# Stores of ScalarE's results and of the block inverses, issued from ScalarE's DMA queue instead of SyncE's

## The chip, the cores and the metric

The kernel runs on one core of a Trainium2 chip. The metric is the time of one execution on the device in microseconds (us), the median of several runs. The core has five engines with instruction streams of their own: TensorE (PE, matrix products), VectorE (DVE), ScalarE (ACT), GpSimd (POOL) and SyncE (SP). Here SyncE does nothing but start DMA transfers. A DMA is an instruction of the engine whose queue issues it: it stands in that engine's order, waits there for what it reads or overwrites, and so holds what stands behind it on that engine.

## The reference

One layer over 512 latent tokens and 256 context tokens, all in float32 with a model width of 1024. A half-step feed-forward block stands at either end; between them stand two parallel mixers, merged by sigmoid gates:

```python
x = ffn_sublayer(x, mod_x, 0, ffn1_w_in, ffn1_w_out)          # post_ln(a*x + 0.5*gate*swiglu(modulate(x)))
ctx = ffn_sublayer(ctx, mod_c, 0, ffn1_w_in, ffn1_w_out)
qa, ka, va, qkv_b, z_b, a_b, b_b, ga, gb = split_proj(modulate(x, shift_x, scale_x) @ w_in)
...
o_a = na_latent(grid(qa), grid(ka), grid(va), kc_h, vc_h, na_rpb)     # 8 heads, 8x16 window and all context keys
o_ctx2, s_ctx = gated_delta_chunks(*gdn_prepare(qkv_c, ...), s0, update_ctx)   # 4 heads x 2 directions
o_lat2, _ = gated_delta_chunks(*gdn_prepare(qkv_b, ...), s_ctx, True)          # chunks of 64 tokens
o_b = gdn_output(o_lat2[0] + jnp.flip(o_lat2[1], axis=2), z_b, gdn_norm_w)
y = sigmoid(ga) * (o_a @ w_pa) + sigmoid(gb) * (o_b @ w_pb)
x = post_ln(a * x + gate_x * (y @ w_o), ln_g[1], ln_b[1])
x = ffn_sublayer(x, mod_x, 2, ffn2_w_in, ffn2_w_out)
```

The recursion (`gated_delta_chunks`) is what the change lies beside. For each chunk it solves a unit lower triangular system, (I + m) uw = rhs with m from `k_beta @ k.T * decay`, and then passes a 128x128 state from chunk to chunk.

## The kernel before

Products with weights are made as three fp32r matmuls of split operands: the high part of the weight `wh` (a cast on ScalarE, L129), its low part `wl` (VectorE, L130), and the activations' parts `uxh` and `uxl` (L183 to L185). The raw weights `wr` are loaded by SyncE some steps ahead (L165).

The order of instructions on each engine is not written out: the program is written in the tile framework, whose scheduler orders every engine's instructions by a timeline of its own from the dependences. A DMA moved from one queue to another is thus planned anew, and other instructions may come out in another order too.

The stretch from about 760 to 1040 us holds the recursion. Its systems are handled in three blocks of two steps (`bi` 0, 1, 2). For each:

- `gram` loads the decays `Dt` (L908, VectorE L911, exponential on ScalarE L912), has the products k k^T and q k^T made by `products`, and forms `Bt` (VectorE L917), which SyncE stores to DRAM as `bd` (L918), and `At` (L921). For steps 2 and 3 `products` copies each product out of PSUM on ScalarE (`kq`, L891), uses it, and stores it to DRAM as `kqd` (L892), from which steps 4 and 5 and the mirrored direction read it again (L896); two `kq` buffers exist.
- `base_inverse` reads the 32x32 diagonal blocks back from `bd`, 64 at once (`Ltr` and `L`, L937), brings one half into order on ScalarE (L938), and inverts them in 31 dependent steps of a product and a reduction on VectorE (`bt` L944, `Xt` L945). Four DMAs store the result to DRAM as `rd` (L949).
- `inverse` loads `rd` again, in another layout, as `T0` and `T1` (L966; the profile calls both `T`), and joins 32x32 blocks to 64x64 and 128x128 by small matmuls (`mm`, L847, into the PSUM tiles `pi`), with copies between them on VectorE (`Y` L988 and L1015, `T` L1004) and ScalarE (L979, L1005, L1023).
- `scan_step` passes the state on: `r`, `vn`, `S`, and the outputs `oacc`.

These steps depend on one another, so they leave TensorE free between. It is filled with the projections of the attention and the gates: the list `FILLS` holds 28 tiles of `qa`, `ka`, `va` (4 each), `ga` and `gb` (8 each), and `turn` hands out quarters of them after each step by the rates `RATE`. Each tile is made by `fill_spill`: 24 matmuls into a PSUM bank (`pm`, two of them), one ScalarE instruction that brings it to `spill` (L595 for qa, L597 for ka and va, L599 for ga and gb, two buffers), and a store of 256 KB to DRAM (L603). The tile `z` is made in the same function, earlier, with a further VectorE instruction.

After the third block `gdn_out` normalizes the recursion's output, turns it on TensorE (L850) and writes it through ScalarE (`vn`, L1107) to `obd` (L1108). `attend` then makes the attention and combines: it loads `ob` from `obd` (L1265) and `z` (L1267).

Of the kernel before, what the change touches and what calls it, by code (L numbers as in the profile page):

```python
# [57 lines left out]
def body(ctx, tc, I, out, dbg=None):  # L58
    nc = tc.nc
# [499 lines left out]
    obd = tl(dp, [4, P, NX], "obd")  # L559
# [25 lines left out]
    def fill_spill(p, name, m, dst, parts=1):  # L585
        w = win_w(name, m)
        px = tl(pm, [P, NX], *PMB)
        for k in range(KT):
            if k and k % (KT // parts) == 0:
                yield  # L590
            mm3k(px[:], w[0], w[1], uxh, uxl, k)
        t = tl(p, [P, NX], "spill", 2)
        if name == "qa":

            S.activation(t[:].rearrange("p (b r c) -> p r b c", b=4, c=16), px[:].rearrange("p (r b c) -> p r b c", b=4, c=16), AF.Copy, scale=0.125)  # L595
        elif name in ("ka", "va"):
            S.copy(t[:], px[:])  # L597
        else:
            S.activation(t[:], px[:], AF.Tanh, scale=0.5)  # L599
        if name == "z":  # L600

            V.scalar_tensor_tensor(t[:], t[:], 1.0, px[:], op0=ALU.add, op1=ALU.mult)
        nc.sync.dma_start(dst[m], t[:])  # L603
        yield


# [271 lines left out]
    def products(p, s):  # L878

        def one(n, a, o):  # L880
            if s == 1:
                return [kk01[p][:, m ^ 2] for m in range(4)]
            if s < 4:
                t = tl(pgq, [P, 4, P], "pq", 2)
                for m, (d, c, i) in enumerate(mats_of(s)):
                    mm(t[:, m, :], kT[2 * p + i][:, c], a[2 * p + i][:, c - o], start=True, stop=True)
                if s == 0:
                    kk01[p] = t
                else:
                    u = tl(gb_, [P, 4, P], "kq", NKQ)  # L890
                    S.copy(u[:], t[:])  # L891
                    nc.sync.dma_start(kqd[n, s - 2, p], u[:].rearrange("p m c -> p (m c)"))  # L892
            else:
                t = tl(gb_, [P, 4, P], "kq", NKQ)
                for h in range(2):
                    nc.sync.dma_start(t[:, 2 * h:2 * h + 2].rearrange("p m c -> p (m c)"), kqd[n, 5 - s, p, :, 256 * (1 - h):256 * (2 - h)])  # L896
# [28 lines left out]
    def base_inverse(bd, rd):  # L925


        L = tl(gb_, [P, 32, 32], "L")
        tr = tl(gb_, [64, 32, 32], "Ltr")
        Xt = tl(gb_, [P, 16, 32], "Xt", 2)  # L930
        G.memset(Xt[:], 0.0)
        for q in range(4):
            G.memset(Xt[32 * q:32 * q + 32].rearrange("p c k -> p (c k)")[:, q % 2:512:34], 1.0)
        st = 32 * P + 32
        for q in range(4):
            dst = tr[32 * q:32 * q + 32] if q < 2 else L[32 * q:32 * q + 32]
            nc.sync.dma_start(dst, bass.AP(bd.tensor, bd.offset + (q // 2) * 8 * MSTR, [[st, 32], [P, 32], [1, 32]]))  # L937
        S.copy(L[0:64].rearrange("p r c -> p c r"), tr[:])  # L938

        G.memset(L[:].rearrange("p r c -> p (r c)")[:, 0:1024:33], -1.0)  # L940
        for i in range(1, 32):
            c = (i + 1) // 2
            t = tl(gb_, [P, 16, 32], "bt")
            V.tensor_tensor(t[:, 0:c, 0:i + 1], L[:, i:i + 1, 0:i + 1].to_broadcast([P, c, i + 1]), Xt[:, 0:c, 0:i + 1], ALU.mult)  # L944
            V.tensor_reduce(Xt[:, 0:c, i], t[:, 0:c, 0:i + 1], AX, ALU.add, negate=True)  # L945
            if i % 4 == 0:
                yield
        for q in range(4):
            nc.sync.dma_start(bass.AP(rd.tensor, rd.offset + (q // 2) * 32 * 1024 + (q % 2) * 32, [[1024, 32], [64, 16], [1, 32]]),  # L949
                              Xt[32 * q:32 * q + 32])  # L950
        yield

# [138 lines left out]
    def gdn_out(p):  # L1091

        oacc = oaccs[p]
        for t2 in range(2):
            o = oacc[:, 2 * t2:2 * t2 + 2].rearrange("p t i c -> p (t i) c")
            sq = tl(gq, [P, 4, P], "r", 2)
            S.activation(sq[:], o, AF.Square)
            ss = tl(gq, [P, 4], "ss", 2)
            V.tensor_reduce(ss[:], sq[:], AX, ALU.add)
            rs = rsqrt_eps(gq, ss[:], 4, 1.0 / 128.0)  # L1100
            V.tensor_tensor(o, o, rs[:, :, None].to_broadcast([P, 4, P]), ALU.mult)
        for i in range(2):
# [4 lines left out]
            S.activation(o, ps[:].rearrange("p t c -> p (t c)"), AF.Copy, scale=nw[:, 0:1])  # L1107
            nc.sync.dma_start(obd[2 * p + i], o)  # L1108

    Sst = [None, None]  # L1110
    res, rds, inv = {}, {}, {}
# [565 lines left out]
```

## Time and profile before

| | us |
|---|---|
| median of 3 runs | 1548.15 |
| lowest and highest | 1546.49, 1550.94 |
| profiled execution, its time | 1550.49 |
| profiled execution, its span | 1548.7 |
| busy: TensorE | 1469.7 (95%) |
| busy: VectorE | 1049.7 (68%) |
| busy: ScalarE | 604.2 (39%) |
| busy: GpSimd | 230.7 (15%) |
| mean granted clock of TensorE | 0.986 |

The busy times come from one profiled execution. In the rows below, a row of the timeline holds its start, its duration, the engine, the line of the kernel, the operation, output and inputs by their names in the program, and the number of instructions that the row groups; the bracket is the idle time of the engine ahead of it and what ended it. `SPq` and `ACTq` are the queues from which SyncE and ScalarE issue DMAs; the duration of such a row is the issue, not the transfer. A row of the waits holds who waited for whom: the total in us, the number of times, the longest one.

### The profile page before, as it was taken

The page shows a single profiled execution, that of the slowest core. Times are in us where ns is not written, and L with a number is a line of the kernel's source. Part 1 is how long each engine was busy: PE and PEld are TensorE (multiplying, and loading weights), DVE is VectorE, ACT ScalarE, POOL GpSimd, SP SyncE. Part 2 cuts the span into 40 slices and gives each one's busy share as a digit, 9 for nine tenths or more (in the row PEclk, how much of TensorE's full clock was granted, in tenths as well). Part 3 has the DMA queues.
Part 4 walks back from the last instruction along what each step waited for, and adds up shares of the span by engine and source line. Part 5 has one row for each costly group of instructions (what it writes and reads, how often), then busy time and mean ns, then how long its engine had stood idle before and what let it go on. Part 6 is the DMA issues. An engine that isn't in the chain of part 4 may idle for free.

```text
span 1548.7 us, 23667 instructions
## 1 busy us (share of the span) xinstructions
PE 1469.7 (95%) x9221; PEld 1259.6 (81%) x9221; DVE 1049.7 (68%) x1792; ACT 604.2 (39%) x1005; POOL 230.7 (15%) x224
## 2 busy tenths in 40 slices
PE   6999999999999999999996899999999999999997
PEld 4779988888888888898874677866677999998886
DVE  8666762577555397768667886666668599887426
ACT  5434321212112245645533344356516454344310
POOL 0000000000000021223301001266432022220001
PEclk9999999999999999999998999999999999999999
DMA  9566563656555533222476534274353133334422
GB/s 323 196 202 206 179 200 98 190 177 207 191 184 180 191 109 127 92 92 86 131 201 183 163 103 120 76 259 127 100 183 135 60 110 123 109 95 151 136 82 82
DMA packets 107586, 230.72 MB, mean 149 GB/s; under 512 B 34177, under 2 KB 47825, under 8 KB 107473
## 3 DMA queue, kind: packets, MB, share of 16 engines
q1 hardware_dynamic: 105312, 221.79, 45.0%
q10 hardware_dynamic: 1586, 5.32, 0.9%
q0 software_dynamic: 576, 2.10, 0.4%
q8 instruction: 72, 1.18, 0.3%
q14 instruction: 40, 0.33, 0.1%
HBM read 206.33 MB, written 22.85 MB: 148 GB/s over the span
## 4 chain that ended last, share of the span: by engine, by line
PE 62%; DMA 15%; DVE 13%; issue 5%; ACT 3%; POOL 1%; SPq 1%; DVEq 0%; ACTq 0%; POOLq 0%
PE ps L202 19%; DMA wr<-in_w_adaT_dram 7%; PE pm L183 5%; PE ps L185 5%; PE ps L183 5%; PE ps L184 5%; PE pm L185 5%; PE pm L184 4%; DVE wl L130 3%; PE ps L1464 3%; PE ps L1466 3%; PE ps L1465 2%; PE pc L847 2%; DVE adap L272 2%; DMA wr<-in_up_dram 1%
## 5 line engine op out<-in xcount | busy, mean ns | idle before, releaser
L130 DVE TENSOR_TENSOR wl<-wr,wh 128x1024 fp32r<-128x1024 f32 (+1 forms) x215 | 263.5, 1230 | 172.0 <-ACT wh L129 171.2
L129 ACT CAST wh<-wr 128x1024 fp32r<-128x1024 f32 (+1 forms) x215 | 217.6, 1017 | 339.6 <-PE ps L202 77.0
L272 DVE SCALAR_TENSOR_TENSOR adap<-wr,crow 128x1024 f32<-128x1024 f32 x112 | 137.0, 1223 | 90.3 <-DMA wr<-in_w_adaT_dram 88.7
L183 PE MATMUL ps<-uxh,wh 128*128 128x512 f32 (+1 forms) x496 | 182.6, 370 | 4.1 <-ACT wh L129 3.9
L185 PE MATMUL ps<-uxh,wl 128*128 128x512 f32 (+1 forms) x496 | 182.3, 368 | 4.3 <-DVE wl L130 4.2
L184 PE MATMUL ps<-uxl,wh 128*128 128x512 f32 (+1 forms) x496 | 181.2, 366 | 1.1 <-DVE uxl L130 1.0
L108 POOL TENSOR_TENSOR rs<-ve,mhalf 128x1 f32<-128x1 f32 (+2 forms) x46 | 52.4, 1142 | 765.0 <-DVE ve L104 762.1
L183 PE MATMUL pm<-uxh,wh 128*128 128x512 f32 x320 | 132.1, 413 | 4.3 <-ACT spill L599 2.3
L185 PE MATMUL pm<-uxh,wl 128*128 128x512 f32 x320 | 127.4, 398 | 0.9 <-DVE wl L130 0.9
L184 PE MATMUL pm<-uxl,wh 128*128 128x512 f32 x320 | 126.4, 395 | 0.0
L185 PEld LDWEIGHTS ps<-uxh,wl 128*128 128x128 f32 x496 | 94.8, 191 | 23.2 <-DVE wl L130 8.6
L183 PEld LDWEIGHTS ps<-uxh,wh 128*128 128x128 f32 x496 | 94.8, 192 | 20.8 <-ACT wh L129 6.7
L184 PEld LDWEIGHTS ps<-uxl,wh 128*128 128x128 f32 x496 | 95.3, 192 | 15.7 <-DVE uxl L130 1.6
L183 PE MATMUL ps<-uch,wh 128*128 128x256 f32 x352 | 98.6, 280 | 0.0
L185 PE MATMUL ps<-uch,wl 128*128 128x256 f32 x352 | 98.3, 279 | 0.0
L184 PE MATMUL ps<-ucl,wh 128*128 128x256 f32 x352 | 98.3, 279 | 0.0
L202 PE MATMUL ps<-wh,hx 128*128 128x512 f32 x352 | 94.8, 389 | 0.0
L202 PEld LDWEIGHTS ps<-wh,hx 128*128 128x128 f32 x352 | 65.9, 188 | 13.6
L183 PEld LDWEIGHTS pm<-uxh,wh 128*128 128x128 f32 x320 | 61.0, 191 | 16.2 <-ACT spill L599 3.2
L185 PEld LDWEIGHTS pm<-uxh,wl 128*128 128x128 f32 x320 | 60.9, 190 | 15.4 <-DVE wl L130 2.2
L129 ACT CAST hx<-fs 128x512 fp32r<-128x512 f32 x22 | 13.6, 620 | 151.0 <-DVE fs L265 151.0
L184 PEld LDWEIGHTS pm<-uxl,wh 128*128 128x128 f32 x320 | 61.0, 191 | 10.3
(411 smaller groups left out, 3494.8 us busy)
## 6 DMA issues: line engine op xcount, KB each, us to landing
wr<-in_w_adaT_dram SPq DMA_DIRECT2D x88, 512.0 KB, 4.3
wr<-in_up_dram SPq DMA_DIRECT2D x80, 512.0 KB, 3.4
wr<-in_dn_dram SPq DMA_DIRECT2D x58, 512.0 KB, 3.5
wr<-in_win_dram SPq DMA_DIRECT2D x52, 512.0 KB, 3.9
rb<-in_up_dram SPq DMA_DIRECT2D x18, 512.0 KB, 4.3
wr<-in_w_o_dram SPq DMA_DIRECT2D x8, 512.0 KB, 3.9
ac<-in_up_dram SPq DMA_DIRECT2D x6, 512.0 KB, 5.3
Dt<-gcd SPq DMA_DIRECT2D x12, 256.0 KB, 5.6
```

The source lines that it names most:

```text
L108: G.tensor_tensor(rs[:], ve[:], mhalf[:, 0:n], ALU.pow)
L129: S.copy(hi, src)
L130: V.tensor_tensor(lo, src, hi.bitcast(F32), ALU.subtract)
L183: T.matmul(ps, a, uh[:, k, :], start=(k == 0), stop=False)
L184: T.matmul(ps, a, ul[:, k, :], start=False, stop=False)
L185: T.matmul(ps, b, uh[:, k, :], start=False, stop=(k == nk - 1))
L202: T.matmul(banks[t][d][:, c0:c1], a[:, sl], b[:, d * 512 + c0:d * 512 + c1], start=first and j == 0, stop=last and j == 2)
L272: V.scalar_tensor_tensor(pr[:], raw[:], 1.0, crow, op0=ALU.mult, op1=ALU.mult, accum_out=col[:, c:c + 1])
L847: last[0] = T.matmul(*a, **k).ins
L1464: T.matmul(ps[:], a, uh[:, k], start=k == 0, stop=False)
L1465: T.matmul(ps[:], a, ul[:, k], start=False, stop=False)
L1466: T.matmul(ps[:], b, uh[:, k], start=False, stop=k == 3)
```

## The change

Four kinds of DMA are issued by ScalarE (`nc.scalar`) that SyncE (`nc.sync`) issued before. What they read and where they write is the same.

```diff
     if name == "z":
         V.scalar_tensor_tensor(t[:], t[:], 1.0, px[:], op0=ALU.add, op1=ALU.mult)
-    nc.sync.dma_start(dst[m], t[:])
+
+    (nc.sync if name == "z" else nc.scalar).dma_start(dst[m], t[:])
     yield
...
     S.copy(u[:], t[:])
-    nc.sync.dma_start(kqd[n, s - 2, p], u[:].rearrange("p m c -> p (m c)"))
+    nc.scalar.dma_start(kqd[n, s - 2, p], u[:].rearrange("p m c -> p (m c)"))
...
     for q in range(4):
-        nc.sync.dma_start(bass.AP(rd.tensor, rd.offset + ..., [[1024, 32], [64, 16], [1, 32]]),
+        nc.scalar.dma_start(bass.AP(rd.tensor, rd.offset + ..., [[1024, 32], [64, 16], [1, 32]]),
                           Xt[32 * q:32 * q + 32])
...
     S.activation(o, ps[:].rearrange("p t c -> p (t c)"), AF.Copy, scale=nw[:, 0:1])
-    nc.sync.dma_start(obd[2 * p + i], o)
+    nc.scalar.dma_start(obd[2 * p + i], o)
```

These are 28 stores of `spill`, 8 of `kq`, 12 of `Xt` (three blocks of four) and 4 of `vn`: 52 DMAs. The first, second and fourth kind store what ScalarE wrote just before; `Xt` is written by VectorE. By the added blank line, the lines from L603 on have a number higher by one in the changed kernel.

The change moves other instructions as well. On SyncE's queue, around the first block inverse, stood before (`Xt_1245` and `rd0` are the first block's inverse, `T1` and `T0` its reload, `L_1365` and `Ltr_1366` the second block's systems, `kq_1438` and `kq_1442` products of the third):

```order
L937 DMA L_1365_7591<-bd1_1277_7043 32x32x32 x2
L949 DMA rd0_1222_6801<-Xt_1245_6934 512x1x32 x4
L603 DMA gbd_894_4996<-spill_1341_7404 128x512
L165 DMA wr_1359_7559<-in_win_dram 128x1024
L896 DMA kq_1438_7951<-kqd_1208_6729 128x256
L966 DMA T1_1347_7433<-rd0_1222_6801 128x4x32
L966 DMA T0_1346_7432<-rd0_1222_6801 128x4x32
L966 DMA T1_1385_7654<-rd0_1222_6801 128x4x32
L966 DMA T0_1384_7653<-rd0_1222_6801 128x4x32
L896 DMA kq_1438_7951<-kqd_1208_6729 128x256
L896 DMA kq_1442_7970<-kqd_1208_6729 128x256 x2
```

At the same place of SyncE's queue stands now:

```order
L909 DMA Dt_1440_7962<-gcd_892_4994 128x2x256
L897 DMA kq_1438_7951<-kqd_1208_6729 128x256
L938 DMA L_1365_7591<-bd1_1277_7043 32x32x32 x2
L897 DMA kq_1438_7951<-kqd_1208_6729 128x256
L165 DMA wr_1359_7559<-in_win_dram 128x1024
L897 DMA kq_1442_7970<-kqd_1208_6729 128x256 x2
L967 DMA T1_1347_7433<-rd0_1222_6801 128x4x32
L967 DMA T1_1385_7654<-rd0_1222_6801 128x4x32
L967 DMA T0_1346_7432<-rd0_1222_6801 128x4x32
L967 DMA T0_1384_7653<-rd0_1222_6801 128x4x32
```

The stores of `rd0` and of the spill are gone from it, and the four `T` loads have moved behind the loads of `kq_1438` and `kq_1442`. On ScalarE stands at that place now:

```order
L599 ACTIVATE spill_1341_7404<-pm_1337_7369 128x512
L129 CAST wh_1343_7409<-wr_1342_7407 128x1024
L604 DMA gbd_894_4996<-spill_1341_7404 128x512
L939 COPY L_1365_7591<-Ltr_1366_7592 64x32x32
L950 DMA rd0_1222_6801<-Xt_1245_6934 512x1x32 x4
L913 ACTIVATE Dt_1440_7962<-Dt_1440_7962 128x512
```

The `rd0` stores have come between the copy of `L_1365`, which waits for `Ltr_1366`, and the exponential of `Dt_1440`; before, the same rows stood there without the two DMA rows and with the cast ahead of the spill. On VectorE, some 20 us later, around the copy `Y6` that TensorE waits for, stood before:

```order
L945 TENSOR_REDUCE Xt_1367_7593<-bt_1406_7827 128x10
L944 TENSOR_TENSOR bt_1407_7830<-L_1365_7591,Xt_1367_7593 128x11x22
L945 TENSOR_REDUCE Xt_1367_7593<-bt_1407_7830 128x11
L944 TENSOR_TENSOR bt_1408_7833<-L_1365_7591,Xt_1367_7593 128x11x23
L945 TENSOR_REDUCE Xt_1367_7593<-bt_1408_7833 128x11
L917 SCALAR_TENSOR_TENSOR Bt_1436_7942<-kq_1437_7943,beta_897_5004,Dt_1435_7935 128x128
L944 TENSOR_TENSOR bt_1409_7836<-L_1365_7591,Xt_1367_7593 128x12x24
L917 SCALAR_TENSOR_TENSOR Bt_1436_7942<-kq_1437_7943,beta_897_5004,Dt_1435_7935 128x128
L1015 COPY Y6_1363_7572<-pi_1357_7541 128x256
L917 SCALAR_TENSOR_TENSOR Bt_1436_7942<-kq_1437_7943,beta_897_5004,Dt_1435_7935 128x128 x2
```

and stands now:

```order
L945 TENSOR_TENSOR bt_1406_7827<-L_1365_7591,Xt_1367_7593 128x10x21
L918 SCALAR_TENSOR_TENSOR Bt_1436_7942<-kq_1437_7943,beta_897_5004,Dt_1435_7935 128x128 x2
L946 TENSOR_REDUCE Xt_1367_7593<-bt_1406_7827 128x10
L1016 COPY Y6_1363_7572<-pi_1357_7541 128x256
L918 SCALAR_TENSOR_TENSOR Bt_1436_7942<-kq_1437_7943,beta_897_5004,Dt_1435_7935 128x128 x2
L918 SCALAR_TENSOR_TENSOR Bt_1441_7969<-kq_1442_7970,beta_897_5004,Dt_1440_7962 128x128 x4
L945 TENSOR_TENSOR bt_1407_7830<-L_1365_7591,Xt_1367_7593 128x11x22
```

`Y6` has moved ahead of five instructions of the second block's inversion (`bt_1407` to `bt_1409`). At the second `Y6` of this block, some 20 us later, it is four in the same way.

More of the change, by code (lines that the diff above doesn't have):

```diff
@@ L948, in base_inverse @@
         for q in range(4):
[L949 removed]
+            nc.scalar.dma_start(bass.AP(rd.tensor, rd.offset + (q // 2) * 32 * 1024 + (q % 2) * 32, [[1024, 32], [64, 16], [1, 32]]),
                               Xt[32 * q:32 * q + 32])
```

## The prediction

> **What bounds the kernel now.** I read the page first (engine totals, chain), then the stretch in which the moved stores lie (760 to 1040 us) by windows, then TensorE's idle gaps and who ended them, then SyncE's queue around each gap.
>
> ```profile
> PE 1469.7 (95%) x9221; PEld 1259.6 (81%) x9221; DVE 1049.7 (68%) x1792; ACT 604.2 (39%) x1005; POOL 230.7 (15%) x224
> 800.00:830.00 30.00, 28.34 (x139) 23.14 (x138) 26.64 (x69) 12.69 (x19) 0.00 (x0) 1.00 0.64 197
> 830.00:860.00 30.00, 15.03 (x159) 10.84 (x157) 21.18 (x69) 9.97 (x18) 5.08 (x14) 0.77 0.57 148
> 860.00:890.00 30.00, 24.91 (x243) 20.07 (x244) 23.56 (x56) 9.15 (x21) 0.00 (x0) 0.94 0.63 181
> 890.00:920.00 30.00, 28.95 (x330) 23.75 (x329) 25.43 (x86) 15.74 (x35) 3.33 (x9) 1.00 0.44 110
> ```
>
> The columns of the windows are length, busy time of TensorE, its weight loads, VectorE, ScalarE and GpSimd, granted clock, DMA share, GB/s. TensorE is 95% busy over the span, but half idle in 830 to 860, at a granted clock of 0.77. ScalarE is busy 10.0 us of those 30, and at most 15.7 in the other rows, so it has room for issues. What idles TensorE:
>
> ```profile
> 846.92 0.69 PE L847 MATMUL pi<-T,Bt 32*32 32x32 f32 x32 [14.58 <-DMA T<-rd]
> 860.74 0.68 PE L847 MATMUL pi<-Tt,Y 64*64 64x64 f32 x16 [1.14 <-DVE Y L1015]
> 875.37 0.68 PE L847 MATMUL pi<-T,Bt 64*64 64x64 f32 x16 [1.42 <-DVE T L1004]
> 881.22 0.68 PE L847 MATMUL pi<-Tt,Y 64*64 64x64 f32 x16 [2.92 <-DVE Y L1015]
> 953.67 0.45 PE L847 MATMUL pi<-T,Bt 32*32 32x32 f32 x32 [0.85 <-DMA T<-rd]
> 955.24 1.26 PE L847 MATMUL pc<-r,Tt 128*128 128x128 f32 x8 [1.12 <-DVE r L1046]
> 958.81 0.42 PE L847 MATMUL pi<-Y,T 32*32 32x32 f32 x28 [0.91 <-DVE Y L988]
> 1021.47 0.82 PE L1245 MATMUL pt<-ident,pr 128*128 128x128 f32 x4 [1.78 <-POOL pr L1241]
> ```
>
> The bracket is the idle time before the row and who ended it. One stall is large: TensorE stands 14.58 us until the first block inverse has been stored (rd<-Xt) and read back (T<-rd). The rest are gaps of 0.9 to 2.9 us, mostly behind VectorE. SyncE's queue and VectorE around the large one:
>
> ```profile
> 832.66 0.69 DVE L945 TENSOR_REDUCE Xt<-bt 128x16 f32<-128x512 f32 x1
> 833.26 1.22 DVE L130 TENSOR_TENSOR wl<-wr,wh 128x1024 fp32r<-128x1024 f32 x1
> 833.59 1.48 SPq L937 DMA_DIRECT2D L<-bd  x2
> 833.76 1.94 ACT L938 COPY L<-Ltr 64x1024 f32<-64x1024 f32 x1 [4.17 <-DMA Ltr<-bd]
> 835.17 5.17 SPq L949 DMA_DIRECT2D rd<-Xt  x4
> 842.71 2.02 SPq L966 DMA_DIRECT2D T<-rd  x4
> 844.77 4.87 SPq L896 DMA_DIRECT2D kq<-kqd  x3
> 842.71 3.86 DMA T<-rd
> 834.09 5.72 DMA L<-bd
> ```
>
> (The last two are rows of the chain of waits.) The inverse is complete at 833.35. Its four stores occupy SyncE from 835.17 to 840.34; 2.4 us later the loads start, and the first lands at 846.57. So 9.4 us pass between the last reduction and the first load's issue, and this is the only place where the store's queue itself lies on TensorE's path for long.
>
> What SyncE waits for in 760 to 1015 us:
>
> ```profile
> SPq L603 <- ACT spill L597: 38.1, 5, 14.2
> SPq L603 <- ACT spill L595: 23.7, 4, 8.9
> SPq L603 <- ACT spill L599: 21.2, 4, 13.1
> SPq L892 <- ACT kq L891: 8.5, 3, 3.6
> SPq L949 <- DVE Xt L945: 7.4, 1, 7.4
> SPq L1108 <- ACT vn L1107: 1.3, 3, 0.8
> ```
>
> These 100.2 us are SyncE's waits for what the moved stores read; of the engines, only those that need a load queued behind them pay. No weight load appears among what ScalarE or TensorE waits for in this stretch, so most of the 100 us cost nothing.
>
> **The change part by part.** Issue prices, minimum/median/maximum in ns:
>
> ```profile
> L500 ACTq DMA_DIRECT2D x1d<-ax x4: 326/330/336, 546.8 to 576.6; - x4
> L949 SPq DMA_DIRECT2D rd<-Xt x12: 561/624/3163, 835.2 to 941.4; - x12
> L1108 SPq DMA_DIRECT2D obd<-vn x4: 319/320/753, 1004.5 to 1012.7; - x4
> ```
>
> *Issues on ScalarE.* 28 stores of spill, 8 of kq and 4 of vn at 0.33 us, and 12 of rd at 0.62 us: 40 x 0.33 + 12 x 0.62 = 20.6 us, taken off SyncE and put on ScalarE over about 280 us. The cover is ScalarE's idle half. Where a copy of a PSUM bank is queued behind a store and TensorE waits for that copy, 0.33 us each time is paid; I take two such places and a few tenths in the attention part: +0.8 us. Bounds: 0 (all hidden) to +3, if the rd stores hold ScalarE as long as 5.17 us in one place.
>
> *First inverse.* On ScalarE the four rd stores stand behind the 1.94 us copy of L (833.76 to 835.70), so they cannot start earlier than on SyncE (835.17) unless the copy does; Ltr is now loaded ahead of fewer other issues, and I take them at about 834 to 838, a little sooner than 835.17 to 840.34. On SyncE the T loads now stand behind the loads of kq, the last of which reuses a buffer that VectorE's product At must first release. Before, that same kq load sat behind T and its wait is in the 4.87 us row. At needs L's landing (5.72 us after the issue, to 839.8) only through the rows queued ahead of it on VectorE; it is then done near 841, and T is issued near 842 where it was 842.71. One T tile of the first pair comes third instead of second, which gives back up to 0.5. Result -0.9 us; bounds -7 (T issued as soon as rd has landed) and +4 (below).
>
> *860 to 882.* VectorE now runs Y and the Bt products ahead of five and four Xt steps. The Xt steps passed:
>
> ```profile
> 858.37 0.42 DVE L944 TENSOR_TENSOR bt<-L,Xt 128x253 f32<-128x253 f32 x1
> 858.83 0.42 DVE L945 TENSOR_REDUCE Xt<-bt 128x11 f32<-128x253 f32 x1
> 877.50 0.58 DVE L944 TENSOR_TENSOR bt<-L,Xt 128x406 f32<-128x406 f32 x1
> 879.34 0.62 DVE L944 TENSOR_TENSOR bt<-L,Xt 128x450 f32<-128x450 f32 x1
> ```
>
> Five at 0.42 is 2.1 us, which covers the 1.14 us gap; four at 0.6 is 2.4, which leaves about half of the 2.92 gap, since kq loads also have to land (bound: all, or nothing). With the 1.42 gap that is -4.0 us, and another -0.5 for matmuls that run at a lower clock after each idle (0.94 in this window against 1.00 later).
>
> *Second inverse.*
>
> ```profile
> 894.91 2.08 SPq L966 DMA_DIRECT2D T<-rd  x4
> 894.91 4.64 DMA T<-rd
> ```
>
> Before, T landed at 899.55, just when TensorE asked for it. TensorE would now ask 5.4 us earlier (0.9 + 4.0 + 0.5). The inverse itself ends earlier by the Xt steps' own shift, about 3.4 us. So a new gap of 2.0 us opens: +2.0. Bounds 0 and +5.4 (the copy of L, queued ahead of the stores on ScalarE, holds them as long as SyncE did).
>
> *Third inverse.*
>
> ```profile
> 946.88 7.67 DMA T<-rd
> 1013.56 5.30 DMA z<-zd
> ```
>
> The last T load was issued at 946.88 behind five attention loads and a store, and took 7.67 us; gaps of 0.85 + 1.12 + 0.91 = 2.9 follow. TensorE's row for it now stands a dozen rows later, behind fill matmuls, so I take two thirds: -2.0, bounds 0 and -2.9.
>
> *End.* The obd stores leave 0.9 us of SyncE ahead of the ob and z loads (z at 1013.56, landing after 5.30 us, on the chain). I take -0.6 of it, bounds -1.8 (the gap at 1021.47) and +1, since ScalarE's store stands behind a square that it must run first.
>
> Sum: +0.8 - 0.9 - 4.5 + 2.0 - 2.0 - 0.6 = -5.2 us. The profiled execution took 1550.49 (span 1548.7), 2.3 over the median of the three runs, 1548.15; 1550.49 - 5.2 = 1545.3 in its terms, 1548.15 - 5.2 = 1543.0 against the median.
>
> **A rule that speaks against it.** The rows: 52 issues at 0.32 to 0.62 us, against landings of 3.86 to 7.67 us. The Trainium skill, page "DMA: Bandwidth & Descriptors", section "Issuing engines are not separate DMA queues", says that DMAs begun by any engine share the same 16 DMA engines, and that a second initiator saves only sequencer time, "usually small relative to the DMA itself". No run yet shows two initiators in this stretch. By that rule the time would be that of the second rival below, 1546 to 1548, where the sum gives 1543.0.
>
> **Rivals.**
> 1. *More: the T loads go as soon as rd has landed.* Nothing on ScalarE holds rd, it is issued by 836 and down by 839, and T goes at 839 instead of 842.71, so the 14.58 us stall shrinks by 3.7 at least, with the rest as above: 1543.0 - 3 - 2 (no gap at the second inverse) - 2 = about 1536. Against it: the kq loads ahead of T on SyncE.
> 2. *Nothing: the transfers set the pace, not the queue.* Of the 100.2 us that SyncE waits, TensorE sees none but the rd stall, where SyncE merely trades rd's 5.17 us for another wait; VectorE's earlier rows are paid back at the second T load (which must wait for 4.64 us of transfer anyway). 0 to -2: 1546 to 1548. It holds if T<-rd is issued at 842 to 843 again and TensorE's gaps only move.
> 3. *Slower: T behind kq behind VectorE.* If L or the first kq half lands as late as the 7.67 us row (against 5.72), At is done near 843, T is issued near 844.5 and lands at 848.4: the first stall grows by 1.9, VectorE's whole later order shifts by as much, and at the second inverse ScalarE's stores behind the copy of L add 3: +5, 1553. It decides from the point where At ends after 841.5.
>
> **How the numbers follow.** Forecast (1538.5 to 1547, two thirds of it below 1543.5) 0.50; rival 1 0.14; rival 2 0.20; rival 3 0.16. A measurement here can tell about 0.3%, 4.6 us. Faster than 1543.5: 0.50 x 0.66 + 0.14 = 0.47. Same: 0.17 + 0.19 = 0.36. Slower: 0.17, with the worst of rival 2's spread. The range for 8 in 10 leaves out the far ends of rivals 1 and 3: 1534 to 1552.
>
> **What would show it.** Right: T<-rd issued near 842 or earlier and the first stall at 13 to 14 us; the gaps at 860, 875 and 881 gone or halved; a gap of about 2 us before the second inverse's matmuls; ScalarE's queue with rd issues of about 0.6 us each. Wrong: a first stall of 15 us or more, a rd issue on ScalarE that waits for microseconds while copies of PSUM wait behind it, or new gaps of TensorE behind ScalarE's spill copies. It would also be wrong if the order of the attention part, which moves by some rows, costs or gains over 2 us.

## The result and the profile after

The changed kernel takes 1564.69 us (median of 4 runs, 1562.16 to 1569.20), the kernel before 1549.55 us (4 runs, 1546.49 to 1553.37): the ratio is 1.0086, 95% interval [1.0056, 1.0115]. By the ratio it is 13 us slower (9 to 18; the medians differ by 15.1), where 1543.0 was forecast and 1534 to 1552 was the range. The profiled execution took 1563.78 us, with a span of 1562.0 us (before 1548.7).

The page's totals of the changed kernel:

```profile
PE 1480.4 (95%) x9221; PEld 1269.3 (81%) x9221; DVE 1048.8 (67%) x1792; ACT 604.3 (39%) x1005; POOL 227.4 (15%) x224
```

Every engine runs as many instructions as before. TensorE is busy for 10.7 us more (1469.7 before) and idle for 2.6 us more (81.6 against 79.0); the mean granted clock is 0.981 (0.986 before). The four windows that the prediction read and two others, in the changed kernel (length, busy time of TensorE, weight loads, VectorE, ScalarE, GpSimd, then granted clock, DMA share, GB/s):

```profile
800.00:830.00 30.00, 28.86 (x144) 23.37 (x143) 24.64 (x73) 11.48 (x17) 0.00 (x0) 1.00 0.61 206
830.00:860.00 30.00, 15.94 (x162) 11.74 (x161) 23.28 (x69) 9.24 (x17) 4.40 (x14) 0.77 0.69 167
860.00:890.00 30.00, 27.17 (x255) 21.94 (x253) 24.61 (x60) 12.08 (x25) 0.00 (x0) 0.94 0.61 183
890.00:920.00 30.00, 28.14 (x298) 22.94 (x296) 23.26 (x78) 14.62 (x33) 3.31 (x9) 1.00 0.43 108
970.00:1000.00 30.00, 28.76 (x295) 25.65 (x291) 14.66 (x36) 6.32 (x17) 4.28 (x6) 0.89 0.08 27
1110.00:1140.00 30.00, 24.76 (x134) 18.68 (x133) 14.71 (x18) 12.47 (x22) 10.44 (x7) 0.89 0.32 89
```

Windows at the same times do not hold the same work, since the recursion began 3.1 us later in this profile. Counted from its start (65 to 125 us), TensorE is busy for 43.1 of the 60 us around the first inverse, for 39.9 before and for 41.5 in a second profile of before (E9, below): it does more in the same time, as forecast. The prediction did not read the last two windows. In the kernel before they are:

```profile
970.00:1000.00 30.00, 29.90 (x280) 26.82 (x279) 18.15 (x41) 7.22 (x16) 5.70 (x9) 1.00 0.19 67
1110.00:1140.00 30.00, 27.43 (x125) 21.07 (x122) 24.73 (x27) 13.25 (x19) 11.42 (x8) 1.00 0.45 141
```

There the granted clock falls from 1.00 to 0.89; counted by the work it is the same (0.90 at 200 to 235 us behind the recursion's start, 0.89 in the tail defined below, 1.00 in both before). TensorE's gaps in the changed kernel, from the timeline (the bracket: idle time before the row, and who ended it):

```profile
849.75 0.65 PE L848 MATMUL pi<-T,Bt 32*32 32x32 f32 x32 [14.06 <-DMA T<-rd]
881.33 0.68 PE L848 MATMUL pi<-Tt,Y 64*64 64x64 f32 x16 [2.69 <-DVE Y L1016]
961.22 0.45 PE L848 MATMUL pi<-T,Bt 32*32 32x32 f32 x32 [0.28 <-DMA T<-rd]
968.30 0.68 PE L848 MATMUL pi<-T,Bt 64*64 64x64 f32 x16 [0.99 <-DVE T L1005]
969.60 0.68 PE L848 MATMUL pi<-Tt,Y 64*64 64x64 f32 x16 [0.62 <-DVE Y L1016]
971.46 2.08 PE L848 MATMUL pc<-r,Tt 128*128 128x128 f32 x8 [0.80 <-ACT Tt L1024]
1029.66 0.55 PE L1215 MATMUL pt<-ident,vst 128*128 128x128 f32 x3 [1.81 <-ACT pT L1248]
1036.86 1.02 PE L1257 MATMUL po<-pT,vw 128*64 128x128 f32 x7 [2.17 <-ACT pT L1248]
1059.81 1.12 PE L1215 MATMUL pt<-ident,vst 128*128 128x128 f32 x4 [2.32 <-ACT pT L1248]
1128.48 0.79 PE L183 MATMUL pm<-oah,wh 128*128 128x512 f32 x1 [3.12 <-ACT wh L129]
```

The gaps of 1.14 and 1.42 us at 860 and 875 have gone; the stall is 14.06 us (14.58 before). New ones stand at 968 to 971, where two joins of the third inverse and the product that takes their result (`Tt`) come close behind one another, in the attention (1029 to 1060), and at 1128, behind a cast of a weight.

Where the time went by stages, in the profiled executions. The *recursion* runs from the first `pq` product to the last `vn` activation, the *attention* to the last copy of `oa`, the *tail* to the first product with `w_o` (`ps<-wh,yh`). The four rows of before and the four of after:

```profile
765.39 1.05 PE L847 MATMUL pq<-kT 128*128 128x128 f32 x8
1011.36 1.27 ACT L1107 ACTIVATE vn<-pc,nw 128x512 f32<-128x512 f32 x2 [1.81 <-PE pc L850]
1110.86 0.69 DVE L1258 COPY oa<-po 128x512 f32<-128x512 f32 x1 [6.58 <-PE po L1256]
1136.61 0.62 PE L202 MATMUL ps<-wh,yh 128*128 128x512 f32 x2
```

```profile
768.46 1.05 PE L848 MATMUL pq<-kT 128*128 128x128 f32 x8
1016.81 1.27 ACT L1108 ACTIVATE vn<-pc,nw 128x512 f32<-128x512 f32 x2 [1.76 <-PE pc L851]
1119.74 0.69 DVE L1259 COPY oa<-po 128x512 f32<-128x512 f32 x1 [6.59 <-PE po L1257]
1149.63 0.62 PE L202 MATMUL ps<-wh,yh 128*128 128x512 f32 x2
```

| us | start | recursion | attention | tail | rest |
|---|---|---|---|---|---|
| before | 765.4 | 246.0 | 99.5 | 25.8 | 412.1 |
| after | 768.5 | 248.4 | 102.9 | 29.9 | 412.4 |

Recursion +2.4, attention +3.4, tail +4.1, rest +0.3, and 3.1 ahead of the changed stretch. The last is chance: a second profile of the kernel before (E9) began the recursion at 770.1. E9 also tells how far one profile can be trusted for a stage: recursion 243.3 against 246.0 and attention 97.0 against 99.5, the same program.

Of the 10.7 us that TensorE is busy for more, 3.1 lie ahead of the recursion and 1.2 behind the tail. The recursion has 4.1 of them (and 1.7 us less of idle time), the attention 0.1 (3.4 us more of idle time), the tail 2.4 (1.8 us more of idle time). E9's total is 1466.4, 3.3 less than the other profile of the same program.

### The profile page after: what moved, and what is told of

Read it like the earlier page. It is cut to its first block, busy times and chain, and to the rows that moved or that the text cites. A ratio compares the mean times of both kernels' runs of the same rounds, so it can differ in the third digit from the quotient of the medians.

```text
span 1562.0 us, 23639 instructions
## 1 busy us (share of the span) xinstructions
PE 1480.4 (95%) x9221; PEld 1269.3 (81%) x9221; DVE 1048.8 (67%) x1792; ACT 604.3 (39%) x1005; POOL 227.4 (15%) x224
## 4 chain that ended last, share of the span: by engine, by line
PE 57%; DMA 18%; DVE 14%; issue 5%; ACT 3%; POOL 1%; SPq 1%; ACTq 0%; DVEq 0%; POOLq 0%
PE ps L202 17%; DMA wr<-in_w_adaT_dram 7%; PE ps L185 4%; PE ps L183 4%; PE ps L184 4%; PE pm L183 4%; PE pm L184 4%; PE pm L185 4%; PE ps L1467 3%; PE ps L1466 3%; PE ps L1465 3%; DVE wl L130 3%; PE pc L848 2%; DVE adap L272 2%; DMA Dt<-gcd 2%
## 5 line engine op out<-in xcount | busy, mean ns | idle before, releaser
L184 PEld LDWEIGHTS ps<-uxl,wh 128*128 128x128 f32 x496 | 94.9, 191 | 15.3 <-DVE uxl L130 1.2
L202 PEld LDWEIGHTS ps<-wh,hx 128*128 128x128 f32 x352 | 65.9, 188 | 14.5 <-DVE fs L265 0.6
```

The lines of the kernel that those rows point to most:

```text
L184: T.matmul(ps, a, ul[:, k, :], start=False, stop=False)
L202: T.matmul(banks[t][d][:, c0:c1], a[:, sl], b[:, d * 512 + c0:d * 512 + c1], start=first and j == 0, stop=last and j == 2)
```

## The experiments

Two things change at once: the queue of 52 stores, and the order in which the scheduler sets other instructions. The experiments separate them. The queue is made a parameter, and an order can be imposed: the program is planned once for other queues, and each engine's instructions are then chained in that plan's order by dependences that only order, and make nobody wait.

```diff
+    queue = lambda kind: nc.scalar if kind in moved else nc.sync
...
+        (nc.sync if name == "z" else queue("spill")).dma_start(dst[m], t[:])
...
+def keep(tc, order):
...
+    last = {}
+    for name, engine in order:
...
+        if engine in last:
+            tc.add_manual_dep(i, last[engine], ..., reason="order")
+        last[engine] = name
```

`MOVED` are the stores on ScalarE's queue, `ORDER_OF` those of the plan whose order is kept. `TAKE` mixes two plans: the order of `BASE`, but in the named pieces (engine, from row to row) that of `OTHER`. *Old order* is the plan with all stores on SyncE, *new order* that of the changed kernel. The line numbers of these kernels are higher by 4 or 5 than those of before. A median is of 5 to 12 executions, beside 23 to 35 of the kernel before.

| | kernel | median us | ratio, 95% interval | recursion | attention | tail |
|---|---|---|---|---|---|---|
| E1 | SyncE, new order | 1562.49 | 1.0084 [1.0056, 1.0111] | 248.3 | 101.4 | 29.4 |
| E2 | ScalarE, old order | 1551.09 | 1.0001 [0.9984, 1.0018] | 240.9 | 100.9 | 25.8 |
| E3 | only rd on ScalarE, planned freely | 1556.79 | 1.0037 [1.0022, 1.0053] | 241.7 | 105.3 | 29.1 |
| E4 | all but rd on ScalarE, planned freely | 1566.27 | 1.0097 [1.0074, 1.0119] | 249.4 | 101.8 | 30.7 |
| E5 | E2 + new tail | 1551.59 | 1.0013 [0.9997, 1.0030] | 242.8 | 98.7 | 28.8 |
| E6 | E2 + new attention | 1556.11 | 1.0048 [1.0029, 1.0067] | 241.1 | 106.1 | 25.9 |
| E7 | E2 + new inverses and scan | 1552.46 | 1.0024 [1.0006, 1.0041] | 248.5 | 97.5 | 25.8 |
| E8 | after + two places in the old order | 1558.51 | 1.0074 [1.0050, 1.0099] | 250.6 | 103.3 | 27.6 |
| E9 | before again | 1548.27 | 0.9999 [0.9982, 1.0016] | 243.3 | 97.0 | 25.6 |
| E10 | old order, rd and kq on ScalarE | 1548.40 | 1.0001 [0.9983, 1.0019] | 245.0 | 97.8 | 25.8 |
| E11 | E2 + new third inverse and scan | 1552.37 | 1.0023 [0.9999, 1.0048] | 244.6 | 102.3 | 28.1 |
| E12 | E6, spill and vn stores on SyncE | 1552.17 | 1.0024 [1.0005, 1.0043] | 241.4 | 103.0 | 27.5 |
| E13 | E2 + new attention, TensorE alone | 1555.83 | 1.0037 [1.0022, 1.0052] | 241.0 | 107.4 | 25.4 |
| E14 | E2 + new attention, all but TensorE | 1555.12 | 1.0032 [1.0014, 1.0050] | 241.5 | 104.7 | 25.8 |
| E15 | E2 + new first two inverses | 1553.16 | 1.0018 [0.9998, 1.0039] | 247.6 | 98.9 | 25.8 |

The stage columns are of the one profiled execution; E13's took 1560.21 us, the slowest of its twelve runs.

### Queue or order: E1 and E2

```diff
 E1: +MOVED = ()                              +ORDER_OF = ('kq', 'obd', 'rd', 'spill')
 E2: +MOVED = ('kq', 'obd', 'rd', 'spill')    +ORDER_OF = ()
```

> All 52 stores are back on SyncE's queue, but every other instruction of each engine is kept in the order that the changed kernel has. Theory O (the loss is the new order of the other instructions): as slow as the changed kernel, 1558 to 1567 us, with the third block's rd stores near 948 and TensorE's wait of about 3 us for a weight cast near 1128. Theory Q (the loss is ScalarE's queue: stores that hold ScalarE or come later from it): back at the kernel before, 1547 to 1552.

> All 52 stores on ScalarE's queue, but every other instruction of each engine is kept in the order that the kernel before has. Theory O: no slower than before, 1543 to 1551 us; the four T loads of the first inverse no longer stand behind any store on SyncE and can go when rd has landed, so that the 14.6 us stall should shrink by 1 to 4 us. Theory Q: 1558 to 1567.

E1 has none of the 52 stores on ScalarE's queue and is as slow as the changed kernel: 1.0084 against 1.0086; its wait for the weight cast is 2.94 us, at 1128.73. E2 has all of them there, in the old order, and is as fast as before. Both times are those of theory O (E2's 1551.09 at the edge of its range), none of theory Q: the loss is the order of the other instructions. The clock goes with it; E1 and then E2, windows as above:

```profile
970.00:1000.00 30.00, 28.10 (x306) 25.07 (x307) 13.89 (x34) 7.01 (x18) 2.86 (x4) 0.89 0.11 40
1110.00:1140.00 30.00, 24.06 (x129) 17.98 (x129) 13.78 (x18) 12.17 (x21) 9.84 (x7) 0.89 0.29 88
```

```profile
970.00:1000.00 30.00, 30.00 (x222) 27.00 (x221) 17.52 (x39) 6.86 (x15) 7.10 (x10) 1.00 0.16 54
1110.00:1140.00 30.00, 27.31 (x124) 20.97 (x121) 24.67 (x27) 13.25 (x19) 11.35 (x8) 1.00 0.43 141
```

E2 also shows what the queue does by itself. Rows of its timeline, first of the inverse, then of the attention:

```profile
845.94 0.65 PE L852 MATMUL pi<-T,Bt 32*32 32x32 f32 x32 [10.78 <-DMA T<-rd]
...
1030.80 0.33 ACTq L608 DMA_DIRECT2D vad<-spill  x1
1031.17 0.59 ACT L1252 COPY pT<-pt 128x512 f32<-128x512 f32 x1 [2.34 <-DMA gt<-gbd]
1031.81 0.48 PE L1261 MATMUL po<-pT,vw 128*64 128x128 f32 x2 [1.91 <-ACT pT L1252]
```

The stall is 10.78 us instead of 14.58 (13.9 in E9), and in the five kernels with all stores on ScalarE and the old order in the recursion (E2, E5, E6, E13, E14) that stage took 240.9 to 242.8 us (241.5 on average), against 246.0 and 243.3 in the two profiles of before: about 3 us less, hardly more than those two differ by. In the attention a copy `pT` stands behind a spill store on ScalarE. The store is issued late, at 1030.80; ScalarE idles 2.34 us, TensorE 1.91 (1.17 in E5 and 0.52 in E7, in the same order). The profile puts that end down to a load of a gate (`gt<-gbd`) that the copy doesn't read.

### Parts of the change, planned freely: E3 and E4

```diff
 E3: +MOVED = ('rd',)
 E4: +MOVED = ('kq', 'obd', 'spill')
```

> Only the 12 stores of Xt to rd are moved to ScalarE; the scheduler plans the rest anew. In its order ScalarE's cast of a w_o weight stands ahead of two casts of w_pa weights, as in the changed kernel. Theory O: the about 4 us between 1118 and 1150 are lost again (wait of about 3 us near 1125), so 1551 to 1560 in all. Theory Q, with the rd stores as the ones that hurt: 1558 to 1567, with the loss around the inverses; if they are not, 1547 to 1552.

> The 28 stores of spill, 8 of kq and 4 of vn are moved to ScalarE, the 12 rd stores stay on SyncE; the scheduler plans the rest anew. The w_o cast stands ahead of the w_pa casts again. Theory O: 4 us lost at 1118 to 1150, and at the inverses what the order there gives, 1551 to 1562. Theory Q, with the rd stores as the ones that hurt: 1546 to 1552; with the other 40: 1558 to 1567.

Each half moved alone is planned anew, and both are slower, by 1.0037 and 1.0097. E3 lies in theory O's range, with a wait of 3.00 us for the cast at 1123.75. E4, 1566.27, lies above theory O's range and in theory Q's for the other 40 stores; E1, with no store on ScalarE, and E2, with all of them, speak against Q, but what E4's own plan costs was not separated from its queue. So the twelve rd stores, which the prediction's gain rests on, don't gain alone either: E3 has the short recursion (241.7) but an attention of 105.3 and a tail of 29.1.

### Which stretch of the new order: E5, E6, E7

```diff
+BASE, OTHER = (), ALL
 E5: +TAKE = {'SP': [(402, 406)], 'Activation': [(728, 735)], 'DVE': [(1248, 1256)]}
 E6: +TAKE = {'SP': [(355, 380)], 'Activation': [(625, 680)], 'DVE': [(1155, 1200)], 'PE': [(5275, 5550)], 'Pool': [(130, 140)]}
 E7: +TAKE = {'SP': [(286, 345)], 'Activation': [(460, 600)], 'DVE': [(720, 1120)], 'PE': [(4560, 5095)]}
```

> Stores on ScalarE, all other instructions in the order of the kernel before, but for one piece after the attention: the cast and the low part of one w_o weight stand ahead of those of two w_pa weights, as in the changed kernel (one row moved on ScalarE, one on VectorE, one load on SyncE). Theory P (the loss is made at several separate places of the order, this one costing 4 us): the distance from the last attention copy (near 1110.8) to the first w_o product grows from 25.8 us to 29 to 30, with a TensorE wait of about 3 us for a weight cast; total 1553 to 1557. Theory C (the loss is made at the inverses and the later gaps follow from it): as the same kernel without this piece, 1551, distance 26.

> Stores on ScalarE, all other instructions in the order of the kernel before, but for the attention stretch (about 1000 to 1110 us), which has the changed kernel's order on all engines. Theory P: the distance from the recursion's last output copy (near 1010) to the last attention copy grows from 101 us to 103 to 105; total 1552 to 1556. Theory C: 1551, distance 101.

> Stores on ScalarE, all other instructions in the order of the kernel before, but for the inverses and the scan (about 790 to 1000 us), which have the changed kernel's order on all engines. Theory P: the recursion's last output copy moves from 1010 to 1015 to 1018, and nothing is lost behind it; total 1554 to 1558. Theory C: the whole loss, 1560 to 1566.

Over E2's 1.0001 the tail adds 0.0012, the attention 0.0047, the inverses 0.0023: 0.0082 together, where the whole order costs 0.0083 (E1) to 0.0086. The sum closes, but loosely: each difference is uncertain by about 0.0025 and the comparison of the two sums by about 0.005. The attention is the largest, though part of it is not in the changed kernel (see E12); the inverses' share is barely clear of nothing, the tail's is not. Each theory P named its stage: the tail 28.8 us (29 to 30 expected), the attention 106.1 (103 to 105), the last output copy of E7 at 1016.1 (1015 to 1018). The times of E5 and E7 are 1.4 and 1.5 us below P's ranges, so what the stages show is larger than what the medians show.

The tail's mechanism is plain, though. ScalarE and SyncE in the kernel before, then in the changed one:

```profile
1114.45 0.33 SPq L165 DMA_DIRECT2D wr<-in_w_o_dram  x1
1115.85 1.14 ACT L129 CAST wh<-wr 128x512 fp32r<-128x512 f32 x2 [1.74 <-PE pm L184]
1117.90 1.05 ACT L129 CAST wh<-wr 128x1024 fp32r<-128x1024 f32 x1 [0.91 <-DMA wr<-in_w_o_dram]
```

```profile
1123.32 0.33 SPq L165 DMA_DIRECT2D wr<-in_w_o_dram  x1
1126.86 2.08 ACT L129 CAST wh<-wr 128x1024 fp32r<-128x1024 f32 x3 [3.88 <-DMA wr<-in_w_o_dram]
```

Before, ScalarE made the two 512-wide casts that TensorE needed next, and then the cast of `w_o`, whose load was under way. Now the cast of `w_o` stands first; ScalarE waits 3.88 us for its load with the two casts behind it, and TensorE 3.12 us for them. With that piece alone moved, E5 shows the wait:

```profile
1119.25 0.50 PE L188 MATMUL pm<-oah,wh 128*128 128x512 f32 x1 [3.00 <-ACT wh L134]
```

### Two places put back: E8

```diff
+BASE, OTHER = ALL, ()
+TAKE = {'SP': [(322, 326), (402, 406)], 'Activation': [(728, 735)], 'DVE': [(1248, 1256)]}
```

> The changed kernel with its own order, but for two small pieces put back as they stood before: on SyncE the load of L for the third block stands ahead of a weight load again (one row), and the w_o weight's cast, low part and a gate load stand behind the w_pa casts again (one row on ScalarE, VectorE and SyncE each). Theory P: the third block's L lands some 3 to 4 us earlier and its inverse ends near 944 in place of 948, of which 0 to 3 us reach the end of the scan; the tail gives back 4: 1557 to 1561 where the changed kernel takes 1564.7. Theory C: the repair at the inverse alone counts, and the tail is 4 us shorter only if the inverse's gain is.

The time, 1558.51 us, lies in P's range. TensorE's wait for the cast has gone, and the tail is 27.6 us instead of 29.9, of the 4 us expected 2.3. Tails in the old order are not all alike, though: 25.4 to 25.9 us in nine profiles, at a granted clock of 1.00, but 28.1 in E11 and 27.5 in E12, at 0.94 as in E8. The other place, the third block's load of `L` put back ahead of a weight load, did nothing: the third inversion ended 181.8 us after the start of the recursion, no earlier than in the changed kernel (179.7; before 174.0), and the recursion took 250.6. Counted from the same start, the load was issued at 123.2 us, in the changed kernel at 124.9 and before at 124.4: the place of this `L` is not the cause.

### The measurement itself, and a smaller change: E9 and E10

E9 is the kernel before with no edit but the parameter; E10 moves rd and kq alone, in the old order.

```diff
 E9:  +MOVED = ()
 E10: +MOVED = ('kq', 'rd')    +ORDER_OF = ()
```

> The kernel before once more, unchanged, to see what one profiled execution and one comparison can tell. The first gram product of the recursion began at 765.4 us in the profiled execution of before and at 765.7 to 770.5 in the nine others, although nothing that is moved runs ahead of it. If that is chance: a ratio of 1 within 0.3%, the start somewhere in 765 to 770, and the stage distances as in the first profile within 1 us: recursion (first gram product to last output copy) 246, attention (to the last attention copy) 99.5, tail (to the first w_o product) 25.7.

> Order of the kernel before on every engine; only the rd and kq stores on ScalarE, those of spill and vn on SyncE. Theory M (with the order held, the stores of rd on ScalarE shorten the recursion by 3 to 5 us, and the stores of spill on ScalarE give 1 to 2 back in the attention, by waiting there for a load's landing ahead of a copy): recursion 241 to 243, attention 99 to 100, in all 2 to 5 us faster than before, ratio 0.997 to 0.999. Rival (the queue does nothing measurable): recursion 245 to 247, ratio 1.000.

Equal programs differ by 0.0001, with an interval of 0.0017 to either side; their stages agree less well than expected, 2.7 and 2.5 us apart instead of 1. E10 gives 1.0001, the rival's outcome, in the recursion as well (245.0). Leaving the spill stores on SyncE keeps the attention at 97.8 us, but the recursion doesn't show the gain of E2; E12, with the same two kinds on ScalarE, has 241.4, so one profile can't tell. No version of the change measurably beat the kernel before.

### The recursion: E11 and E15

```diff
+BASE, OTHER = (), ALL
 E11: +TAKE = {'DVE': [(945, 1120)], 'PE': [(4745, 5095)], 'Activation': [(560, 600)], 'SP': [(330, 345)]}
 E15: +TAKE = {'DVE': [(720, 940)], 'PE': [(4560, 4625)], 'Activation': [(460, 560)], 'SP': [(286, 328)]}
```

> All 52 stores on ScalarE, order of the kernel before, but for the stretch of the third block's inverse and of the scan behind it (about 895 to 1000 us), which has the changed kernel's order on VectorE, TensorE, ScalarE and SyncE. If the later place of the third block's inversion steps among VectorE's other work is what the new order costs in the recursion: its last reduction ends 5 to 7 us later counted from the start of the recursion (175 to 177 us behind the first gram product in place of 170), and the recursion takes 246 to 248 in place of 241. Rival (the loss lies in the first two blocks' order): 240 to 242.

> All 52 stores on ScalarE, the order of before, but from the first to the second block's inversion every engine in the new order; the third block, the attention and the tail in the old one. Theory O3 (the loss in the recursion is the third block's order alone, 1.0023 in the run that had only that one new): 1.000 or just below, recursion 240 to 243 us. Rival (it lies in all three blocks): 1.001 to 1.003, recursion 245 to 248 us.

The theory that the third block's order is the whole of it fell: E11 has 1.0023 and a recursion of 244.6 us (246 to 248 expected), E15 1.0018 and 247.6, the rival's outcome, against 240.9 in E2. Neither ratio is clear of 1 alone; both stages are longer.

What moves with the stage is the end of the third inversion on VectorE. Counted from the recursion's start, its last reduction ends at 169.9 us in E2, at 175.6 in E11 (175 to 177 expected), 174.9 in E15, 178.2 in E7 and 179.7 in the changed kernel; in the two profiles of before at 174.0 and 172.1. In all seventeen profiles the recursion ends 69 to 73 us behind it. In E15 the delay begins with the first inversion, which ends at 70.7 us instead of 67.0. That the later place of the inversion's steps among VectorE's other work delays it is what E11 was made to test, and the end of its third inversion agrees.

VectorE's waits for the loads of `Dt` are not the cause, though they are long in E15. From 780 to 1000 us, E2, then E15, then E13, which has E2's order there (total, times, longest):

```profile
DVE Dt L916 <- DMA Dt<-gcd: 13.6, 7, 3.1
DVE Dt L916 <- DMA Dt<-gcd: 19.7, 8, 5.0
DVE Dt L916 <- DMA Dt<-gcd: 19.3, 8, 5.3
```

E13 waits as long as E15, and its recursion takes 241.0 us; E7 waits 14.5 us and takes 248.5; the changed kernel has 15.4 us of these waits, the kernel before 15.3.

In the third block the changed kernel's gaps (968 to 971, above) are of 0.99, 0.62 and 0.80 us; the window behind them:

```profile
970.00:980.00 10.00, 9.21 (x153) 8.14 (x149) 3.60 (x11) 3.73 (x12) 0.00 (x0) 0.66 0.01 2
```

The granted clock is 0.66 there: in steps of 2 us it reads 1.00 up to 970, then 0.68, 0.50, 0.50 and 0.61, and 1.00 again from 978. The eight products `pc<-r,Tt` behind the third gap take 2.08 us, where eight took 1.26 us at 955.24 before. In the kernel before, the same two joins stood with products of the scan between them, without a gap, and the clock stayed at 1.00 (the window 970 to 1000 above):

```profile
974.52 0.68 PE L847 MATMUL pi<-T,Bt 64*64 64x64 f32 x16
975.13 1.16 PE L847 MATMUL pc<-vn,At 128*128 128x128 f32 x8
977.52 1.05 PE L847 MATMUL pc<-S,kT 128*128 128x128 f32 x8
978.50 0.68 PE L847 MATMUL pi<-Tt,Y 64*64 64x64 f32 x16
```

The Trainium skill's page "TensorE: Matmul & The Clock Gate", section "Why this matters for your kernels", asks for no idle gaps over about 3 us between bursts. The rows here show the clock lower after shorter ones: three gaps under 1 us each, within 5 us. The same three gaps (0.60 to 0.99 us) and a clock of 0.90 to 0.93, at 200 to 235 us behind the recursion's start, stand in all five kernels that have the new order of the third block (the changed one, E1, E7, E8, E11); the other twelve have 1.00 there, E3 with two gaps of 0.59 and 0.47 us. A single gap of 1.5 to 1.7 us at the third inverse (E2, E5, E6, E13, E14) left the clock at 1.00 too. That the gaps brought it down is read from this and from their order in time; no run changed them alone. Nor is a loss by it seen in this stage: the five with the low clock end the recursion 68.6 to 70.2 us behind the third inversion, the others 69.1 to 72.7.

### The attention: E12, E13, E14

```diff
+BASE, OTHER = (), ALL
 E12: E6 with +MOVED = ('kq', 'rd')
 E13: +TAKE = {'PE': [(5275, 5550)]}
 E14: +TAKE = {'SP': [(355, 380)], 'Activation': [(625, 680)], 'DVE': [(1155, 1200)], 'Pool': [(130, 140)]}
```

> As the run with the old order and the new attention (recursion 241, attention 106), but the stores of spill and vn on SyncE again; rd and kq stay on ScalarE. If the 6.0 us stall of TensorE near 1027 there came from the va store that waited on ScalarE's queue ahead of a copy: that stall falls to 0 to 2 us and the attention takes 100 to 102.5. If it came from the order alone: the stall stays at 4 to 6 and the attention at 104 to 107.

> All 52 stores on ScalarE, the order of before, but in the attention part TensorE alone has the new order (its score, transpose and value products); ScalarE, VectorE, GpSimd and SyncE keep the old one there. With all five engines new this piece gave 1.0048 [1.0029, 1.0067]. Theory T (TensorE's new order sets transposes directly ahead of the value products that need their copies, so that it waits for ScalarE): the ratio is 1.004 to 1.005 again, attention stage 103 to 106 us where the old order had 97 to 101. Theory S (the loss is ScalarE's and SyncE's order, where a spill store waits ahead of the copies of the probabilities): 1.000 to 1.001, attention 98 to 101 us.

> The counterpart: all 52 stores on ScalarE, in the attention part ScalarE, SyncE, VectorE and GpSimd have the new order, TensorE the old one. Theory T: 1.000 to 1.001, attention stage 98 to 101 us. Theory S: 1.004 to 1.005, attention 103 to 106 us, with a wait of TensorE of several us near 1027 behind a copy of the probabilities. If both halves give 1.002 to 1.003, the loss is in neither order alone.

The same place in E6, with the spill store on ScalarE, and in E12, with it on SyncE:

```profile
1026.37 0.33 ACTq L608 DMA_DIRECT2D vad<-spill  x1
1026.74 1.07 ACT L1252 COPY pT<-pt 128x512 f32<-128x512 f32 x2 [3.98 <-DMA bias<-in_na_bias_dram]
1027.38 1.97 PE L1219 MATMUL pt<-ident,vst 128*128 128x128 f32 x8 [6.00 <-ACT pT L1252]
```

```profile
1024.41 1.97 PE L1219 MATMUL pt<-ident,vst 128*128 128x128 f32 x8 [1.19 <-ACT pT L1252]
1025.00 0.32 SPq L608 DMA_DIRECT2D vad<-spill  x1
```

On ScalarE the store holds the copy `pT` until 1026.74, and TensorE waits 6.00 us; on SyncE TensorE waits 1.19 us there. The attention is 3.1 us shorter (103.0, just above the 100 to 102.5 expected), still above the 97.0 to 102.3 us of the kernels with the old order in it, and the ratio is 1.0024 against 1.0048, a difference of about its uncertainty (0.0027). So the queue and the new order meet at this place: in E2's order the same store costs 1.91 us. The changed kernel does not have this stall. There the same store is issued 0.45 us behind the end of its copy:

```profile
1028.65 0.33 ACTq L604 DMA_DIRECT2D vad<-spill  x1
```

TensorE's longest wait for a `pT` in the changed kernel's attention is 2.32 us (2.29 in E1, with the store on SyncE). E6 mixes two plans, and a part of its 0.0047 belongs to the mixture: its attention grew by 5.2 us over E2's, the changed kernel's by 3.4 over before.

Which engine's order costs the rest was not one or the other. TensorE's alone gave 1.0037, the four others' alone 1.0032: nearly the third outcome named, "in neither order alone". Their sum, 0.0067 over E2, is more than the 0.0047 of both together, but by less than the uncertainty of the comparison (0.0035). In E13 TensorE waits 2.03 us for a `pT` at 1034.05, which stands behind the store as in E2, where the same product waits 1.91; this does not tell what TensorE's order costs. In E14 ScalarE comes late to what TensorE has next: `pr` stands behind the store, which goes at 1024.77, and TensorE waits 2.92 us for it at 1026.70. That the orders of the engines fit each other only in one plan is a reading of these results, not shown by a run.

## Why the prediction was wrong

*The step that failed* is the limit that the prediction set to the change. Its sum ends at the `z` load near 1020 us, and all rows that moved elsewhere were costed at nothing. It named the possibility ("It would also be wrong if the order of the attention part, which moves by some rows, costs or gains over 2 us") and gave it neither a term nor a chance. The attention's order cost 3.4 us in the changed kernel by the stages; E6 puts it at 7 (0.0047), with a stall that the changed kernel does not have. Of the tail nothing was said; it cost 3 to 4 us by the stages, 2 by the ratio (E5, within its uncertainty). Nor was the later order of the recursion taken as a cost: +3.6 us by the ratio, 7.5 by the stage (E7 against E2). With the stores left on SyncE the new order by itself gives 1.0084 (E1), about the whole of the loss.

*Issues on ScalarE, +0.8.* The kind is right, the price is another. What is paid is not the 0.33 us of the issue but the wait of the store, behind which ScalarE's copies stand: one store in the attention costs 1.91 us in the old order (E2) and 6.00 against 1.19 in E6's mixture. In the changed kernel the queue's part is small, 1.0086 against 1.0084 in E1.

*First inverse, -0.9.* In the changed kernel `T` is issued 77.9 us after the recursion's start, before at 77.3 (75.8 in E9): no gain, and the stall is 14.06 us, just outside the 13 to 14 named. The inversion ends at 70.6 us there (68.0 before), and the last thing that the `T` loads wait for is the landing of `rd` (the last row, of the waits in 835 to 850 us):

```profile
844.15 0.69 DVE L922 TENSOR_TENSOR At<-kq,Dt 128x512 f32<-128x512 f32 x1
844.87 0.80 SPq L897 DMA_DIRECT2D kq<-kqd  x2
846.35 2.02 SPq L967 DMA_DIRECT2D T<-rd  x4
SPq L967 <- DMA rd<-Xt: 0.6, 1, 0.6
```

In the old order (E2) `T` goes at 73.0 us and the stall is 10.78: the first rival's direction, hidden by the new order.

*860 to 882, -4.5.* Two of three gaps went as forecast; the third is 2.69 us, not halved from 2.92. Together the gaps shrank by 2.8 us, where 4.0 was taken.

*Second inverse, +2.0, and third, -2.0.* TensorE's new gap behind `T` is 0.61 us (at 902.82), not 2.0. The third inverse's first gaps shrank (0.28 us behind `T`, 0.85 before), but its last joins brought 2.4 us of new ones and the low clock.

*End, -0.6.* No such gain is to be seen in an attention stage that grew by 3.4 us.

The direct part, with the order held, is about 3 us off the recursion by the stages (E2 and its kin), against the -5.2 of the whole sum, and nothing in all: 1.0001 [0.9984, 1.0018], an interval of nearly 3 us to either side. The attention gives back a part: 99.7 us on average with the spill stores on ScalarE and the old order in it (E2, E5, E7, E11, E15), 98.1 with them on SyncE (the two profiles of before, E10). That is the second rival's time, though not its mechanism. The Trainium skill's page "DMA: Bandwidth & Descriptors", section "Issuing engines are not separate DMA queues", says that a second initiator saves only the time of issuing; E2's ratio agrees. The third rival had the right sign but the wrong place. Its condition was met: `At` ends 76.4 us after the recursion's start, which is 841.8 on the clock of before, later than its 841.5, and the `kq` loads go right behind. But `T` then waits 0.6 us more for `rd`, and the first stall did not grow.

*Open:* which rows of the attention's order cost most, since halves of it cost about as much as the whole; which of VectorE's rows delay the inversions; what the low clock costs; and why the old order suits the chip better in all three stretches than plans made for the same program with other queues (E3, E4 and the changed kernel are all slower).

## What to carry to other kernels

Where a scheduler sets the order, moving a DMA to another queue is two changes: the queue, and a new plan of everything behind it, to the end of the program. Compare the two orders over their whole length and give each displaced stretch a term with a bound, or hold the order fixed and measure the queue alone. In these runs a store on a computing engine cost its wait, not its issue: see what stands behind it there, and who waits for that.

## What the runs showed of the hardware that was not expected

Low clock after short gaps: three gaps of 0.62 to 0.99 us within 5 us were followed by a granted clock of 0.50 from 972 to 976 us (0.66 over 970 to 980) and eight products of 2.08 us, and a low clock stands there in every kernel with that order and in none of the others. A single gap of 1.5 to 1.7 us was not.

A store on ScalarE's queue was held until a load that it has no data in common with had landed, if the profile's releaser is right (`gt<-gbd` in E2, 2.34 us of ScalarE's idle time; `bias` in E6, 3.98 us). In E6 the times fit: the load was issued at 1019.15, landed 7.1 us later, at 1026.25, and the store went at 1026.37. In E2 they fit less: by the one landing that the profile has, 6.2 us, the loads issued at 1022.4 and 1022.8 were down by 1029.0, and the store went at 1030.80. The store was issued 4.4 us behind the end of its copy in E6, 2.0 us in E12, on SyncE's queue, where nothing that TensorE needed stood behind it, and 0.45 us in the changed kernel. Why the store or the copy waits was not tested.
